# A gate block between two attention heads, half of two convolution channels by ScalarE and accumulating transfers, and a PSUM bank change in the last neighbourhood pair

## The chip, the cores and the metric

The kernel runs on one core of a Trainium2 chip. The metric is the device time of one execution in microseconds, as a median over repeated runs; beside it stands one execution that was taken with the hardware profiler. Engines are named as in the profile: PE (TensorE matmul), PEld (TensorE weight load), DVE (VectorE), ACT (ScalarE), POOL (GpSimd) and SP (SyncE, which issues most transfers). Times inside the profiled execution are microseconds from the start of its span. The two layers of the network are called the first and the second layer.

## The reference

The reference is a trunk of two layers over x of 512 tokens by 1024 channels. In each layer three token mixers run side by side on the same normalised input, a gate for each mixes them, and a SwiGLU FFN and a per-layer input embedding follow:

```python
h = rmsnorm(x, norm_mix[i])
proj = h @ w_in[i]
qa, ka, va, glu_in, qc, kc, vc, gates = jnp.split(proj, SPLITS, axis=-1)
ya = diff_attention(qa, ka, va, ...)          # 4 heads, two softmaxes each, a1 - lam * a2, then rmsnorm
yb = conformer_conv(glu_in, conv_w[i], ...)   # GLU, depthwise convolution of 31 taps over 512 channels, layernorm, silu
yc = neighbourhood_attention(qc, kc, vc, rpb[i])   # 8 heads, an 8 x 16 window on an 8 x 64 grid
ga, gb, gc = jnp.split(jax.nn.sigmoid(gates), 3, axis=-1)
merged = ga * (ya @ w_br_a[i]) + gb * (yb @ w_br_b[i]) + gc * (yc @ w_br_c[i])
x = x + merged @ w_o[i]
...
```

What matters here is the stretch of a layer from the neighbourhood attention to the gates: the convolution's depthwise taps are elementwise work that can run beside the matmuls at any time before `yb` is needed.

## The kernel before

Activations lie with channels on the 128 partitions and the 512 tokens along the free axis, so a projection's output block is a tile of 128x512 in one PSUM bank. Every fp32 product is emulated: both operands are split into a high and a low part in the fp32r type, and `mm3` (L181 to L183) issues three matmuls for each 128-deep chunk. A block of 1024 inputs is 8 chunks, 24 matmuls. Weights come in on SP's queue (`weights`, three buffers ahead), ACT copies the high part (L147) and DVE subtracts it for the low part (L161), so each weight tile puts about one 128x1024 instruction on ACT and on DVE. The helpers `split`, `tt`, `stt` and `act` record everything under their own lines: L147 is any ACT instruction, L161 any DVE tensor_tensor, L164 any DVE scalar_tensor_tensor; the tile names tell them apart.

PE runs its instructions in program order, and that order is written by hand: `layer` calls the blocks one after the other (`natten_in`, `natten_v`, `diff_in`, `diff_v`, `gate_c` and so on), and work that depends on softmax results is put into generators (`natten_unit`, `diff_unit`, `norm`) that are advanced by `tick`, once for every four chunks (twelve matmuls) that any projection issues. A `yield 2` means: go on two ticks later. So the pieces of one attention head stand a fixed number of matmuls apart among the projections of other blocks. On the other engines the order comes from the tile scheduler.

A head of the difference attention (`diff_in`, then four `diff_unit`s) does this: projections for Q and K, rope on DVE (tiles `diff_rp`: two multiplications, an addition and a split for each of Q and K), scores into `diff_sc`, a maximum on DVE (L910), two exponentials on ACT (`diff_a`, `diff_e`), the difference of the two on DVE (`diff_a`, L164), eight transposes on PE (L867, into two banks named `diff_tr`), their split by ACT and DVE into `diff_pt`, and the products with the values into `diff_av`. At the end of a head `norm` transposes the squares (L217), DVE sums them (L220, `diff_sm`), POOL raises to a power (L227, `diff_rc`), and PE transposes the result back over all partitions (L231) into a bank of the same two `tr` banks that the attention transposes use. PSUM has three `mm` banks, two `sc`, two `tr` and one `av`.

A neighbourhood unit ends in eight matmuls with the values (L752). Its result goes to the bank `av` for the first head of a pair and to an `mm` bank for the second; DVE then reads it into `natten_y`. `natten_v` projects the values; its four accumulators take two `mm` banks, the `av` bank and an `sc` bank, and eight reads by ACT and DVE (`natten_v`, `natten_x`) empty them.

The depthwise convolution has 4 channel blocks (`zs`) of 31 taps in a layer, one DVE instruction for each tap (L549 for the first of a block, then L164 into `conv_z`). `taps` yields them one by one, `background(after, n)` places n of them behind a given instruction (the table `BG` holds n for each kind of block), and `conv` issues those that are left. The accumulating form of a transfer is already in use in the FFN, where POOL adds one weight tile onto another (L995).

## Time and profile before

| what | value |
|---|---|
| median of 3 runs | 1779.75 us (1779.65 to 1779.84) |
| the profiled execution | 1779.11 us, of which its span is 1777.3 us and 1.8 us lie around it |
| mean granted clock of PE in it | 0.998 |
| PE, PEld | 1760.8 us (99%), 1544.1 us (87%) |
| DVE | 1413.5 us (80%), 2354 instructions |
| ACT | 893.4 us (50%), 1529 instructions |
| POOL | 97.4 us (5%), 114 instructions |
| transfers | 258.12 MB, mean 145 GB/s |

PE's durations overlap: a matmul of 128x512 is listed with 389 ns, but the next one starts about 227 ns after it (the modelled end reaches into the next), so PE's busy share hides short waits. Where a wait is measured here between two starts, the usual distance between them is taken off.

### The profile page before, as it was taken

To read this page: it belongs to the slowest core of one execution; us is meant where nothing else is said; L and a number is where in the kernel's file an instruction comes from. 1 tells how busy PE (TensorE), PEld (TensorE's weight loads), DVE (VectorE), ACT (ScalarE), POOL (GpSimd) and SP (SyncE) were. 2 spreads that over 40 slices of the span, in tenths; PEclk is the share of its full clock that TensorE was granted. 3 is DMA by queue.
4 is the path that set the end of the run, shared out by engine and by line. 5 is a ranking of instruction groups with operands and counts; after the bars stand their busy time and mean duration, and the time that the engine had idled before them with its cause. 6 is when DMAs were issued, how large, how long until landed. Compare 5 with 4: busy or idle time off the path is not lost.

```text
span 1777.3 us, 26765 instructions
## 1 busy us (share of the span) xinstructions
PE 1760.8 (99%) x9954; PEld 1544.1 (87%) x9954; DVE 1413.5 (80%) x2354; ACT 893.4 (50%) x1529; POOL 97.4 (5%) x114
## 2 busy tenths in 40 slices
PE   9999999999999999999999999999999999999998
PEld 7888878888899899998888887888888998989987
DVE  7967887998898587787776688779887985877776
ACT  5576555325565254454545765452356643534444
POOL 0000000000111010100000000000001110101000
PEclk9999999999999999999999999999999999999999
DMA  6577541334757366544446765423256673655332
GB/s 224 162 186 186 170 132 43 110 99 139 227 156 190 113 166 158 137 124 128 154 134 174 183 177 156 115 67 99 94 172 202 176 178 111 178 135 159 99 104 95
DMA packets 113698, 258.12 MB, mean 145 GB/s; under 512 B 14496, under 2 KB 23456, under 8 KB 113568
## 3 DMA queue, kind: packets, MB, share of 16 engines
q1 hardware_dynamic: 100176, 232.03, 42.7%
q0 software_dynamic: 12672, 23.07, 8.2%
q8 instruction: 78, 1.28, 0.3%
q10 hardware_dynamic: 720, 1.31, 0.2%
q14 instruction: 52, 0.43, 0.1%
HBM read 218.60 MB, written 7.34 MB: 127 GB/s over the span
## 4 chain that ended last, share of the span: by engine, by line
PE 90%; DVE 5%; ACT 1%; DMA 1%; issue 1%; SPq 0%; POOL 0%; ACTq 0%; DVEq 0%; POOLq 0%
PE ffn_mm L1025 4%; PE ffn_mm L1027 4%; PE ffn_mm L181 4%; PE ffn_mm L183 4%; PE ffn_mm L182 4%; PE ffn_mm L1026 4%; PE ffn_sc L1027 3%; PE ffn_sc L1025 3%; PE ffn_sc L1026 3%; PE mergea_mm L181 2%; PE mergea_mm L183 2%; PE mergea_mm L182 2%; PE gateb_mm L181 2%; PE wo_mm L181 2%; PE wo_mm L183 2%; PE wo_mm L182 2%
## 5 line engine op out<-in xcount | busy, mean ns | idle before, releaser
L164 DVE SCALAR_TENSOR_TENSOR conv_z<-glu_z,pre_par,conv_z 128x512 f32<-128x512 f32 x240 | 179.3, 747 | 3.0
L147 ACT ACTIVATE ffn_wh<-ffn_wr 128x1024 fp32r<-128x1024 f32 (+1 forms) x92 | 92.7, 1014 | 111.3 <-PE ffn_mm L182 80.7
L161 DVE TENSOR_TENSOR ffn_wl<-ffn_wr,ffn_wh 128x1024 fp32r<-128x1024 f32 (+1 forms) x92 | 107.3, 1172 | 5.4 <-ACT ffn_wh L147 4.9
L995 POOL DMA_DIRECT2D ffn_qk<-w_fu x88 | 77.9, 980 | 603.3 <-DMA ffn_qk<-w_fu 299.6
L161 DVE TENSOR_TENSOR ffn_t<-ffn_mm,wo_rb 128x512 f32<-128x512 f32 (+1 forms) x64 | 38.6, 604 | 67.8 <-PE ffn_mm L183 67.8
L147 ACT ACTIVATE mergea_wh<-mergea_wr 128x1024 fp32r<-128x1024 f32 (+1 forms) x32 | 27.1, 848 | 91.2 <-PE mergea_mm L182 71.7
L147 ACT ACTIVATE ffn_wh<-ffn_qk 128x1024 fp32r<-128x1024 f32 x44 | 46.7, 1061 | 36.7 <-PE ffn_mm L182 16.0
L161 DVE TENSOR_TENSOR ffn_wl<-ffn_qk,ffn_wh 128x1024 fp32r<-128x1024 f32 x44 | 53.8, 1223 | 10.8 <-ACT ffn_wh L147 10.8
L161 DVE TENSOR_TENSOR ffn_t<-ffn_t,ffn_t 128x512 f32<-128x512 f32 (+1 forms) x46 | 31.3, 680 | 32.0 <-ACT ffn_t L147 31.5
L161 DVE TENSOR_TENSOR diff_wl<-diff_wr,diff_wh 128x1024 fp32r<-128x1024 f32 x32 | 39.1, 1221 | 18.0 <-ACT diff_wh L147 12.4
L181 PE MATMUL ffn_mm<-ffn_v,ffn_wh 128*128 128x512 f32 x132 | 51.4, 389 | 0.0
L182 PE MATMUL ffn_mm<-ffn_v,ffn_wh 128*128 128x512 f32 x132 | 51.4, 389 | 0.0
L183 PE MATMUL ffn_mm<-ffn_v,ffn_wl 128*128 128x512 f32 x132 | 51.3, 389 | 0.0
L181 PE MATMUL ffn_mm<-ffn_y,ffn_wh 128*128 128x512 f32 x132 | 51.3, 389 | 0.0
L182 PE MATMUL ffn_mm<-ffn_y,ffn_wh 128*128 128x512 f32 x132 | 51.3, 389 | 0.0
L183 PE MATMUL ffn_mm<-ffn_y,ffn_wl 128*128 128x512 f32 x132 | 51.3, 389 | 0.0
L910 DVE TENSOR_REDUCE diff_s<-diff_sc 128x1 f32<-128x512 f32 x64 | 42.4, 683 | 10.0 <-PE diff_sc L819 10.0
L147 ACT ACTIVATE natten_e<-natten_e,natten_s 128x192 f32<-128x192 f32 (+1 forms) x88 | 39.3, 473 | 21.8 <-DVE natten_s L715 18.9
L1027 PE MATMUL ffn_mm<-wo_h,ffn_wl 128*128 128x256 f32 x176 | 49.8, 283 | 0.0
L1027 PE MATMUL ffn_sc<-wo_h,ffn_wl 128*128 128x256 f32 x176 | 49.8, 283 | 0.0
L1026 PE MATMUL ffn_mm<-wo_h,ffn_wh 128*128 128x256 f32 x176 | 49.8, 283 | 0.0
L1026 PE MATMUL ffn_sc<-wo_h,ffn_wh 128*128 128x256 f32 x176 | 49.8, 283 | 0.0
(882 smaller groups left out, 6477.3 us busy)
## 6 DMA issues: line engine op xcount, KB each, us to landing
ffn_qk<-w_fu POOLq DMA_DIRECT2D x88, 256.0 KB, 5.7
ffn_wr<-w_fg SPq DMA_DIRECT2D x44, 512.0 KB, 3.8
ffn_wr<-w_fd SPq DMA_DIRECT2D x32, 448.0 KB, 3.8
ffn_r<-w_fu SPq DMA_DIRECT2D x44, 256.0 KB, 4.3
ffn_qk<-w_fg SPq DMA_DIRECT2D x44, 256.0 KB, 4.0
ffn_qk<-w_fu SPq DMA_DIRECT2D x44, 256.0 KB, 4.4
natten_wr<-w_in SPq DMA_DIRECT2D x16, 512.0 KB, 4.1
diff_wr<-w_in SPq DMA_DIRECT2D x16, 512.0 KB, 3.8
```

Source lines behind the costliest of these rows:

```text
L147: i = self.nc.scalar.activation(out, in_, func, **kw)
L161: return self.nc.vector.tensor_tensor(out, a, b, op)
L164: return self.nc.vector.scalar_tensor_tensor(out, a, s, b, op0, op1)
L181: mm(out, wh, ah, start=first, stop=False)
L182: mm(out, wh, al, start=False, stop=False)
L183: mm(out, wl, ah, start=False, stop=last)
L910: nc.vector.tensor_reduce(out=m[:, u:u + 1], in_=sc, op=ALU.max, axis=AX.X, negate=True)
L995: nc.gpsimd.dma_start(q, wu[:, lo], accum_op=ALU.add)
L1025: mm(out, wh[:, c], bh, start=first and k == 0, stop=False, skip_group_check=True)
L1026: mm(out, wh[:, c], bl, start=False, stop=False, skip_group_check=True)
L1027: mm(out, wl[:, c], bh, start=False, stop=k == 3, skip_group_check=True)
```

## The change

Four things change, in both layers.

1. The second gate c block (`gate_c(acc, 1)`) is called between `diff_in(2)` and `diff_in(3)` instead of behind both. On PE the number of instructions stays (9745 rows); the 24 matmuls of that block now stand where the first projection of the last head stood, and that head's projections come 24 matmuls later.
2. For the third and fourth channel block of the convolution (`far`), the first nine taps each leave DVE. ACT multiplies the input by the tap (`conv_t`, 128x512; the first tap with the bias goes straight into the accumulator `conv_b`), and POOL issues a transfer from SBUF to SBUF that adds `conv_t` onto `conv_b` (256 KB, L575 of the changed kernel). That is 18 ACT instructions and 16 transfers in a layer; DVE's `taps` starts these two blocks at the tenth tap. `link` issues the next of the 18: two with each gate c block and one around each of two places between the heads.
3. The numbers of taps behind other blocks change: four instead of three at each weight tile of `natten_v`, none instead of one in the rope of a head, one instead of two at a gate c block, three instead of four in the merge.
4. In the last neighbourhood pair the second head's result goes to the `av` bank, like the first's, instead of to an `mm` bank.

Line numbers of the changed kernel are by 1 higher in the helpers (L161 is L162) and by 30 to 32 from `natten_unit` on (L867 is L899).

```diff
-BG = dict(glu=2, natten=1, values=3, diff=1, gatec=2, branchc=2, gateb=4, mergea=4, mergea2=2)
+BG = dict(glu=2, natten=1, values=4, diff=0, gatec=1, branchc=2, gateb=4, mergea=3, mergea2=2)
+LINKS = 18
...
-        self.todo = self.taps(zs, cs)
+        self.todo, self.links = self.taps(zs, cs), self.chain(zs)
...
         self.diff_in(2, sd, ya)
+        self.link()
+        self.gate_c(acc, 1)
         self.diff_in(3, sd, ya)
-        for m in range(1, KD):
+        self.link()
+        for m in range(2, KD):
             self.gate_c(acc, m)
...
-            c = self.sb("z", [P, 512])
+            if j < 2:
+                c, n = self.sb("z", [P, 512]), 0
+            else:
+                for _ in self.links:
+                    pass
+                c, n = self.far[j - 2], LINKS // 2
             cs.append(c)
-            for d in range(CON3W):
+            for d in range(n, CON3W):
...
+    def chain(self, zs):
+
+        self.far = [self.sb("b", [P, 512]) for _ in range(2)]
+        for n in range(LINKS):
+            d, j = divmod(n, 2)
+            w = self.par(self.i, "cw", (j + 2) * CON3W + d)
+            src = zs[j + 2].rearrange("p a b -> p (a b)")[:, d * GR:d * GR + 512]
+            if d == 0:
+                self.act(self.far[j], src, AF.Identity, scale=w, bias=self.par(self.i, "cb", j + 2))
+            else:
+                t = self.sb("t", [P, 512])
+                self.act(t, src, AF.Copy, scale=w)
+                self.nc.gpsimd.dma_start(self.far[j], t, accum_op=ALU.add)
+            yield
+
+    def link(self):
+
+        ph, self.phase = self.phase, "conv"
+        next(self.links, None)
+        self.phase = ph
...
-        av = self.ps(("av", "mm")[u])
+        av = self.ps("mm" if u and pr < 3 else "av")
...
         self.background(self.act(acc[m], ps, AF.Copy), self.bg["gatec"])
+        self.link()
+        self.link()
```

How the scheduler now places this is seen at three places. The first is DVE in the first layer, from the end of the first head's `norm` input to the two evacuations of the attention transposes (`diff_pt`). The names ending in 2139 and 2230 (`diff_rp`) are the ropes of the last head's Q and K. Before:

```order
L164 SCALAR_TENSOR_TENSOR diff_s_2278<-diff_s_2278,glu_nlam_445,diff_sm_1804 128x1
L161 TENSOR_TENSOR gatec_wl_2487<-gatec_wr_2485,gatec_wh_2486 128x1024
L161 TENSOR_TENSOR diff_rp_2139<-diff_rp_2139,diff_kh_2151 128x512
L161 TENSOR_TENSOR diff_rp_2230<-diff_rp_2230,diff_r_1315 128x512
L164 SCALAR_TENSOR_TENSOR conv_z_2147<-glu_z_324,pre_par_67,conv_z_2147 128x512
L161 TENSOR_TENSOR diff_rp_2231<-diff_rp_2231,diff_r_1317 128x512
L164 SCALAR_TENSOR_TENSOR diff_a_2283<-diff_e_2289,diff_s_2278,diff_a_2283 128x512
L161 TENSOR_TENSOR diff_rp_2230<-diff_rp_2230,diff_rp_2231 128x512
L161 TENSOR_TENSOR diff_pt_2311<-diff_tr_2306,diff_pt_2311 128x512
L161 TENSOR_TENSOR diff_pt_2319<-diff_tr_2314,diff_pt_2319 128x512
```

The same place after, from the sum of squares on (`diff_sm_2265`, L221):

```order
L221 TENSOR_REDUCE diff_sm_2265<-diff_tr_2260 128x4
L162 TENSOR_TENSOR diff_rp_2141<-diff_rp_2141,diff_r_1319 128x512
L162 TENSOR_TENSOR diff_rp_2142<-diff_rp_2142,diff_r_1321 128x512
L165 SCALAR_TENSOR_TENSOR diff_sm_2267<-diff_sm_2265,diff_sm_2225 128x4
L942 TENSOR_REDUCE diff_s_2271<-diff_sc_2272 128x1
L162 TENSOR_TENSOR diff_rp_2141<-diff_rp_2141,diff_rp_2142 128x512
L942 TENSOR_REDUCE diff_s_2271<-diff_sc_2278 128x1
L162 TENSOR_TENSOR diff_rp_2141<-diff_rp_2141,diff_kh_2151 128x512
L162 TENSOR_TENSOR gatec_wl_2501<-gatec_wr_2499,gatec_wh_2500 128x1024
L947 RECIPROCAL diff_s_2271<-diff_s_2271 128x1
L162 TENSOR_TENSOR diff_pt_2304<-diff_tr_2299,diff_pt_2304 128x512
```

One rope instead of two and no tap stand ahead of the first `diff_pt` now, and the difference `diff_a` of the next scores has moved behind both of them.

The second place is DVE at the end of `natten_v` in the first layer, where the accumulators are emptied (`natten_v`, `natten_x`; `conv_z_370` is the first block of the convolution). Before, from the first accumulator in an `mm` bank on:

```order
L161 TENSOR_TENSOR natten_v_697<-natten_mm_562,natten_v_697 64x4x128
L164 SCALAR_TENSOR_TENSOR conv_z_370<-glu_z_321,pre_par_67,conv_z_370 128x512
L161 TENSOR_TENSOR glu_wl_840<-glu_wr_838,glu_wh_839 128x1024
L161 TENSOR_TENSOR natten_v_697<-natten_mm_561,natten_v_697 64x4x128
L161 TENSOR_TENSOR natten_v_699<-natten_sc_564,natten_v_699 64x4x128
L161 TENSOR_TENSOR natten_v_698<-natten_mm_562,natten_v_698 64x4x128
L161 TENSOR_TENSOR natten_v_698<-natten_av_563,natten_v_698 64x4x128
L161 TENSOR_TENSOR natten_x_701<-natten_sc_564,natten_x_701 64x4x128
```

And after:

```order
L162 TENSOR_TENSOR natten_v_701<-natten_mm_562,natten_v_701 64x4x128
L165 SCALAR_TENSOR_TENSOR conv_z_370<-glu_z_321,pre_par_67,conv_z_370 128x512
L162 TENSOR_TENSOR glu_wl_844<-glu_wr_842,glu_wh_843 128x1024
L165 SCALAR_TENSOR_TENSOR conv_z_370<-glu_z_321,pre_par_67,conv_z_370 128x512
L162 TENSOR_TENSOR natten_v_701<-natten_mm_561,natten_v_701 64x4x128
L165 SCALAR_TENSOR_TENSOR conv_z_370<-glu_z_321,pre_par_67,conv_z_370 128x512
L162 TENSOR_TENSOR natten_v_703<-natten_sc_564,natten_v_703 64x4x128
L165 SCALAR_TENSOR_TENSOR conv_z_370<-glu_z_321,pre_par_67,conv_z_370 128x512
L162 TENSOR_TENSOR natten_v_702<-natten_mm_562,natten_v_702 64x4x128
L162 TENSOR_TENSOR natten_wl_925<-natten_wr_923,natten_wh_924 128x1024
L165 SCALAR_TENSOR_TENSOR conv_z_370<-glu_z_321,pre_par_67,conv_z_370 128x512
L162 TENSOR_TENSOR natten_x_705<-natten_sc_564,natten_x_705 64x4x128
```

Four taps and a weight split now stand between the weight split of `glu` and the last read of the `sc` bank, where four reads stood; one read (of the `av` bank) has moved behind it. In the second layer the eight reads stand in the same order as before, with no tap among them.

The third place is POOL's queue in the first layer. Before, the power of `glu`'s norm and those of the four heads (`diff_rc`) followed one another:

```order
L227 TENSOR_TENSOR glu_rc_317<-glu_sm_315,pre_power_104 128x4
L227 TENSOR_TENSOR diff_rc_2276<-diff_sm_2274,pre_power_104 128x4
L227 TENSOR_TENSOR diff_rc_2580<-diff_sm_2578,pre_power_104 128x4
L227 TENSOR_TENSOR diff_rc_2865<-diff_sm_2863,pre_power_104 128x4
L227 TENSOR_TENSOR diff_rc_3153<-diff_sm_3151,pre_power_104 128x4
```

After, up to the second head's power (`conv_b_1867` and `conv_b_1868` are the two accumulators):

```order
L575 DMA conv_b_1867<-conv_t_2163 128x512
L575 DMA conv_b_1868<-conv_t_2233 128x512
L575 DMA conv_b_1867<-conv_t_2236 128x512
L575 DMA conv_b_1868<-conv_t_2423 128x512
L228 TENSOR_TENSOR diff_rc_2269<-diff_sm_2267,pre_power_104 128x4
L575 DMA conv_b_1867<-conv_t_2492 128x512
L575 DMA conv_b_1868<-conv_t_2495 128x512
L575 DMA conv_b_1867<-conv_t_2566 128x512
L575 DMA conv_b_1868<-conv_t_2569 128x512
L228 TENSOR_TENSOR diff_rc_2600<-diff_sm_2598,pre_power_104 128x4
```

Each transfer waits for the landing of the one before it on the same accumulator and for its own ACT instruction. The first head's power stands behind four transfers, the second head's behind eight, the third head's behind all sixteen, and so does the fourth's. On ACT, the instructions for transfers two to six (`conv_t_2233` to `conv_t_2495`) stand five in a row right behind the two that read the first head's `diff_av` (`diff_ss`, `diff_t`). The `conv_t` tiles share their seven buffers with `diff_t`, so later ones wait until an earlier transfer has landed.

## The prediction

> **What bounds the kernel now.** The page first: PE is busy for nearly the whole span, so only its waits can be won.
>
> ```profile
> span 1777.3 us, 26765 instructions
> PE 1760.8 (99%) x9954; PEld 1544.1 (87%) x9954; DVE 1413.5 (80%) x2354; ACT 893.4 (50%) x1529; POOL 97.4 (5%) x114
> L164 DVE SCALAR_TENSOR_TENSOR conv_z<-glu_z,pre_par,conv_z 128x512 f32<-128x512 f32 x240 | 179.3, 747 | 3.0
> ```
>
> The span is 1777.3 us of an execution of 1779.11 us. The change moves about 18 taps a layer off DVE, 2 x 18 x 0.747 = 26.9 us of DVE time. That is worth nothing by itself: DVE is at 80%, and what counts is where PE waits for DVE. So next the waits of PE:
>
> ```profile
> PE diff_tr L231 <- DVE diff_pt L161: 6.0, 2, 3.0
> PE diff_mm L614 <- DVE natten_y L161: 1.1, 2, 0.7
> PE natten_mm L752 <- ACT diff_wh L147: 1.0, 2, 0.5
> PE diff_tr L867 <- DVE diff_a L164: 0.9, 2, 0.5
> PE gateb_mm L181 <- ACT gateb_kh L147: 0.3, 2, 0.2
> PE natten_av L752 <- DVE natten_a L161: 0.3, 1, 0.3
> ```
>
> All lie in the stretch that the change touches, most of them once in each layer, and they add up to 9.6 us. That is the most that can be won beside the clock. The largest is the transpose of the first head's `norm` (L231). PE's timeline there, in the first layer:
>
> ```profile
> 220.02 0.60 PE L217 MATMUL diff_tr<-pre_ident,diff_ss 128*128 128x128 f32 x4
> 227.32 0.39 PE L182 MATMUL gatec_mm<-glu_h,gatec_wh 128*128 128x512 f32 x1
> 227.55 0.39 PE L183 MATMUL gatec_mm<-glu_h,gatec_wl 128*128 128x512 f32 x1
> 230.95 0.62 PE L231 MATMUL diff_tr<-pre_ident,diff_rc 128*128 128x128 f32 x4 [3.02 <-DVE diff_pt L161]
> ```
>
> Matmuls start 0.23 us apart (227.32 to 227.55), so L231 could have started at 227.78 and lost 230.95 - 227.78 = 3.17 us. It waits for a `tr` bank, which is free when DVE has done the first `diff_pt`. What DVE did between the sum of squares (start 220.65) and that:
>
> ```profile
> 220.65 0.69 DVE L220 TENSOR_REDUCE diff_sm<-diff_tr 128x4 f32<-128x512 f32 x1 [1.42 <-PE diff_tr L217]
> ...
> 225.25 1.23 DVE L161 TENSOR_TENSOR gatec_wl<-gatec_wr,gatec_wh 128x1024 fp32r<-128x1024 f32 x1
> 226.39 0.68 DVE L161 TENSOR_TENSOR diff_rp<-diff_rp,diff_kh 128x512 fp32r<-128x512 f32 x1
> 226.99 0.68 DVE L161 TENSOR_TENSOR diff_rp<-diff_rp,diff_r 128x512 f32<-128x512 f32 x1
> 227.59 0.74 DVE L164 SCALAR_TENSOR_TENSOR conv_z<-glu_z,pre_par,conv_z 128x512 f32<-128x512 f32 x1
> ...
> 230.12 1.28 DVE L161 TENSOR_TENSOR diff_pt<-diff_tr,diff_pt 128x512 fp32r<-128x512 f32 x2
> ```
>
> DVE has no gap there: its queue, not a dependence, sets 230.12. An instruction of 128x512 costs 0.60 us from start to start (226.39 to 226.99), a tap 0.67, a weight split 1.14. Last the granted clock (third field from the end), in the first layer's wait and behind the second layer's:
>
> ```profile
> 228.00:232.00 4.00, 1.05 (x7) 0.99 (x8) 4.00 (x8) 0.63 (x1) 0.00 (x0) 1.00 0.88 204
> 1109.50:1113.00 3.50, 3.29 (x10) 2.83 (x11) 3.10 (x6) 1.39 (x3) 0.00 (x0) 0.53 0.86 238
> ```
>
> Both layers wait equally long, but only behind the second wait does PE run 3.5 us at 0.53: that costs up to 3.5 x 0.47 = 1.6 us.
>
> **The change part by part.**
>
> *The first head's stall.* In the new order DVE has, between the same sum of squares and the first `diff_pt`: four rope steps, two maxima, one weight split and two small instructions. From 220.65: seven instructions of 0.60 (the sum of squares with them) and the small one make 224.9, if nothing holds them. But the last rope step and the weight split wait for ACT, which now takes `diff_a`, `diff_kh`, the weight copy, `diff_e` and `diff_pt` in that order. ACT's prices and the start of its chain:
>
> ```profile
> 217.15 0.28 PE L183 MATMUL diff_av<-diff_pt,diff_v 128*128 128x256 f32 x1
> 217.47 0.60 ACT L147 ACTIVATE diff_ss<-diff_av 128x512 f32<-128x512 f32 x1
> 217.96 0.68 ACT L147 ACTIVATE diff_t<-diff_av,glu_subg 128x512 f32<-128x512 f32 x1
> 218.53 0.60 ACT L147 ACTIVATE diff_rp<-diff_mm 128x512 f32<-128x512 f32 x1
> 221.98 0.69 ACT L147 ACTIVATE diff_a<-diff_sc,diff_s 128x512 f32<-128x512 f32 x1 [2.85 <-DVE diff_s L910]
> ...
> 222.66 0.68 ACT L147 ACTIVATE diff_e<-diff_sc,diff_s 128x512 f32<-128x512 f32 x1
> ...
> 224.15 1.06 ACT L147 ACTIVATE gatec_wh<-gatec_wr 128x1024 fp32r<-128x1024 f32 x1 [0.73 <-ACT diff_e L147]
> ```
>
> The five `conv_t` run from 218.5, 0.56 us apart, until 221.4, before the first maximum is there. That maximum ends at about 223.2; then `diff_a` 0.68 (221.98 to 222.66), `diff_kh` 0.56, the copy 1.0, `diff_e` 0.68 and `diff_pt` 0.6 give 226.7, and DVE's half of `diff_pt` 0.68 more: 227.4. PE arrives at 227.78. There are eight hand-overs between ACT and DVE, which cost some hundredths each, so I leave 0.2 us of the 3.17: 2 x -2.97 = **-5.9**. Bounds: 0 and 0.8 us left in each layer, so -6.3 to -4.7. The gate block behind `diff_in(2)` costs PE nothing: the same 24 matmuls in another place.
>
> *The clock.* With the wait gone the slow stretch should go: **-1.4**, between -1.6 and 0 (another wait could set it off). The Trainium skill ("TensorE: Matmul & The Clock Gate", Part 1) says that the throttle judges activity in free-running windows of 3413 ns and knows only half and full rate. By that rule the first layer's equal wait was lucky in its phase, so a wait of 3 us that comes back could cost the clock twice; the trace's 0.53 over 3.5 us agrees.
>
> *The last neighbourhood pair.* L614, the projection of the values, waits for `natten_y` because it gets the `mm` bank that the pair's second head used. Now it doesn't: **-1.1** (0 to -1.5). In exchange the second head waits for the single `av` bank. In the first layer DVE reads that bank out by 171.3 and the next product starts at 174.53:
>
> ```profile
> 170.61 0.69 DVE L161 TENSOR_TENSOR natten_y<-natten_y,natten_av 64x512 fp32r<-64x512 f32 x1
> 174.53 0.88 PE L752 MATMUL natten_mm<-natten_pt,natten_v 128*128 128x256 f32 x6
> ```
>
> so nothing is lost.
>
> *The difference `diff_a` before L867.* Two taps stand ahead of it before, 1.3 us, and none after; the wait of 0.9 in two should go: **-0.9** (-0.3 to -0.9). The waits at L752 and at gate b stay, since as much is moved in front of them as is taken away.
>
> *Four taps more in the first layer's `natten_v`.* Here the change adds to DVE where DVE is full:
>
> ```profile
> 74.83 1.22 DVE L161 TENSOR_TENSOR glu_wl<-glu_wr,glu_wh 128x1024 fp32r<-128x1024 f32 x1
> ...
> 78.96 0.69 DVE L161 TENSOR_TENSOR natten_x<-natten_sc,natten_x 64x512 fp32r<-64x512 f32 x1
> 81.13 0.28 PE L711 MATMUL natten_sc<-natten_qk 128*128 128x256 f32 x1
> ...
> 956.96 0.69 DVE L161 TENSOR_TENSOR natten_x<-natten_sc,natten_x 64x512 fp32r<-64x512 f32 x1
> 960.56 0.31 PE L711 MATMUL natten_sc<-natten_qk 128*128 128x256 f32 x1
> ```
>
> The second half of the first scores (L711, 81.13) needs the `sc` bank that `natten_x` empties. After `glu_wl` (done at 76.05) now come four taps, three reads and a weight split: 4 x 0.67 + 3 x 0.72 + 1.14 = 6.0 (a read is 0.69 long), so `natten_x` starts at 82.0 and ends at 82.7: PE waits 1.55 us. The later wait of 0.3 at L752 should vanish in that: **+1.25** (0.5 to 2.0). In the second layer the reads keep their order and end 3 us ahead of PE (956.96 against 960.56): nothing.
>
> *The accumulating transfers.* POOL's queue is otherwise empty, but the heads' powers now stand behind transfers. The nearest rows are the FFN's accumulating transfers, of the same 256 KB, and the power:
>
> ```profile
> L995 POOL DMA_DIRECT2D ffn_qk<-w_fu x88: 862/883/1243, 453.9 to 1643.7; - x88
> DMA to landing us min/median/max: 3.9/5.7/8.6
> L227 POOL TENSOR_TENSOR diff_rc<-diff_sm,pre_power x8: 1006/1007/1017, 222.1 to 1199.3; 128x4 f32<-128x4 f32 x8
> ```
>
> With a landing time D: the second transfer is issued when its `conv_t` is done, at 219.1; the fourth waits for that landing and holds POOL 0.9 us; then the power takes 1.0. It is ready at 221.0 + D, for the median at 226.7, 1.1 us ahead of PE. So **0**, and from D = 6.8 on a wait. I take the median, since the weight stream loads the transfer engines no less in the FFN. The Trainium skill ("DMA: Bandwidth & Descriptors", Anatomy of one DMA) gives 2.0 us plus bytes over 436 GB/s, an estimate of 2.6 us here. By that page the power would be ready 4 us early; the rows above are twice as slow, and I go by them. DVE's tail of the convolution has no wait of PE, and the last landing is long past when DVE goes on from it.
>
> The sum: -5.9 - 1.4 - 1.1 - 0.9 + 1.25 = -8.05. From 1779.11 this is 1771.1; the median lies 0.64 above the profiled execution, so **1771.7**. The best ends of all terms give -6.3 - 1.6 - 1.5 - 0.9 + 0.5 = -9.8 (1769.9), the worst -4.7 + 0 + 0 - 0.3 + 2.0 = -3.0 (1776.8).
>
> **The rivals.** (The bound of no change is 0.2%, 3.56 us, about what a measurement of this kernel can tell.)
>
> *A: POOL's queue takes the place of DVE's.* For: 5.7 us is a median, and 8.6 occurs; the transfers form a chain, and a transfer behind a slow one starts late. At D = 8.6 the first head waits 1.8 us in each layer: 1771.7 + 3.6 = 1775.3. It ends on the other side when the third head's power is late as well:
>
> ```profile
> 251.45 0.28 PE L183 MATMUL diff_av<-diff_pt,diff_v 128*128 128x256 f32 x1
> 293.58 0.49 PE L231 MATMUL diff_tr<-pre_ident,diff_rc 128*128 128x128 f32 x3
> ```
>
> With the first stall gone, these fall 3.2 us earlier. The ninth transfer goes at about 250.5 after the second head's product, four landings follow one after another, then two issues and the power: 250.5 + 4D + 2.8, needed at 290.4. That decides from D = 9.3. At D = 10 it is 2 x 3.2 for the first head and 2 x 2.9 for the third: 1771.7 + 12.2 = 1783.9, slower; at 12 some 1803. Against: no row of 88 is over 8.6.
>
> *B: the stall only moves.* ACT is a chain of hand-overs now; if `diff_e` or the weight copy comes late, L231 waits 2 us instead of 0.2, and the slow clock may stay: 1771.7 + 3.6 + 1.4 = 1776.7. For: by my working the chain ends only 0.4 us ahead of PE. Against: DVE's own work would be done by 226.1 (224.9, a weight split of 1.14 and a small one), so one late hand-over is not added to a full queue.
>
> *C: a wait that the trace of before doesn't show*, for instance a gate c weight tile that now is due 24 matmuls earlier on SP's queue, eats most of it: 1777 to 1782.
>
> **How the numbers follow.** The forecast 0.62 (1769.9 to 1776.8, almost all of it faster); B 0.13, half of it within the bound; A up to D = 9.3 0.10, mostly still faster; A beyond 0.08, slower; C 0.07, mostly within the bound. Faster: 0.60 + 0.06 + 0.08 = 0.74; slower 0.08 + 0.02 = 0.10; the same 0.16. The range leaves out A beyond and part of C on top, and on the low side whatever I haven't seen: 1768.5 to 1779.5.
>
> **What would show it.** L231 leaves the list of PE's waits or stands there with under 0.5 us each; a new line of `natten_sc` on DVE `natten_x` of 1 to 2 us, once; no stretch at 0.5 of the clock behind the first head; landings of the new transfers near 5.7 us. A wait of L231 on POOL `diff_rc` would make A right, a wait on `diff_pt` of 2 us B. A time over 1779.5 would make the sum wrong, not its sizes.

## The result, and the profile after

The changed kernel takes 1776.63 us (median of 18 runs, 1774.15 to 1778.3), beside 1779.27 us for the kernel before on the same chips (18 runs). The ratio is 0.9984, with a 95% interval of 0.9977 to 0.9991: 2.6 us faster, 0.16%, where 8 us were forecast. The profiled execution took 1777.74 us, 1.1 over its median, with a span of 1775.9.

The waits of PE after (engine, line, what it waited for; us in all, times, longest):

```profile
PE diff_av L183 <- DVE diff_pt L162: 1.9, 2, 1.2
PE natten_sc L741 <- DVE natten_x L162: 1.7, 1, 1.7
PE diff_sc L851 <- ACT diff_e L148: 1.5, 2, 0.9
...
PE natten_mm L782 <- DVE natten_a L162: 0.9, 2, 0.5
PE diff_tr L232 <- DVE diff_pt L162: 0.8, 2, 0.4
PE diff_mm L182 <- DVE natten_y L162: 0.5, 2, 0.3
```

The three waits that the sum took away are gone: the first head's L231 (6.0 us), L614 (1.1) and L867 (0.9). The line of L232 that still stands there is another head's. Around the first head's transpose, PE's, DVE's and POOL's timelines of the first layer:

```profile
229.60 0.39 PE L184 MATMUL diff_mm<-glu_h,diff_wl 128*128 128x512 f32 x1
229.83 0.60 PE L232 MATMUL diff_tr<-pre_ident,diff_rc 128*128 128x128 f32 x4
...
228.81 0.67 DVE L162 TENSOR_TENSOR diff_pt<-diff_tr,diff_pt 128x512 fp32r<-128x512 f32 x1
...
227.00 1.39 POOL L228 TENSOR_TENSOR diff_rc<-diff_sm,pre_power 128x4 f32<-128x4 f32 x1
```

L232 follows the matmul before it by the usual 0.23 us. DVE had freed the bank at 229.48, 0.35 us ahead of PE, and POOL's power was ready at 228.4, 1.4 us ahead. But five waits of the list are new: `diff_av`, `natten_sc`, `diff_sc` on ACT's `diff_e`, L232 in the second head, and L182 on `natten_y`. With `natten_sc` the clock came along. Windows of the changed kernel (the granted clock is the third field from the end):

```profile
82.00:86.00 4.00, 3.96 (x13) 3.27 (x14) 3.89 (x13) 2.56 (x9) 0.00 (x0) 0.60 0.57 193
1106.00:1110.00 4.00, 4.00 (x21) 3.21 (x20) 4.00 (x10) 2.19 (x5) 2.00 (x3) 1.00 1.03 209
```

The slow stretch of the second layer is gone, and in this execution one has come up in the first layer, behind the new wait.

Counted from start to start of PE's matmuls (with the usual distance taken off, both layers together), the two profiles compare so:

| place | before | after |
|---|---|---|
| first head's L231 | 6.35 | 0 |
| value projection waits for `natten_y` (L614) | 1.46 | 0 |
| L867 waits for `diff_a` | 1.26 | 0 |
| L752 waits for `natten_a` (first layer, first unit) | 0.45 | 0 |
| `natten_sc` waits for `natten_x` (first layer) | 0 | 1.87 |
| `diff_av` waits for `diff_pt`, second head | 0 | 2.17 |
| `diff_sc` waits for `diff_e`, first head | 0 | 1.86 |
| second head's L232 waits for `diff_pt` | 0 | 1.14 |
| `diff_mm` waits for `natten_y` of the third pair | 0 | 0.87 |
| half clock behind a wait | about 1.6 | about 1.6 |

The last row comes from comparing the slowed matmuls with the same ones at full clock (in the other layer before, in the kernel with the bank undone after). Beside it, 9.5 us went and 7.9 came. That is the 1.4 us by which the spans differ, to within a fraction.

### The profile page after: what moved, and what is told of

Same layout as the page of the kernel before. It is cut to its first block, busy times and chain, and to the rows that moved or that the text cites. A ratio compares the mean times of both kernels' runs of the same rounds, so it can differ in the third digit from the quotient of the medians.

```text
span 1775.9 us, 26835 instructions
## 1 busy us (share of the span) xinstructions
PE 1761.1 (99%) x9954; PEld 1542.6 (87%) x9954; DVE 1392.7 (78%) x2318; ACT 913.0 (51%) x1565; POOL 126.7 (7%) x146
## 4 chain that ended last, share of the span: by engine, by line
PE 91%; DVE 4%; DMA 2%; ACT 1%; issue 1%; SPq 1%; POOL 0%; ACTq 0%; DVEq 0%; POOLq 0%
PE ffn_mm L1057 4%; PE ffn_mm L1059 4%; PE ffn_mm L182 4%; PE ffn_mm L183 4%; PE ffn_mm L184 4%; PE ffn_mm L1058 4%; PE ffn_sc L1059 3%; PE ffn_sc L1057 3%; PE ffn_sc L1058 3%; PE mergea_mm L184 2%; PE mergea_mm L182 2%; PE mergea_mm L183 2%; PE gateb_mm L182 2%; PE wo_mm L182 2%; PE wo_mm L184 2%; PE wo_mm L183 2%
## 5 line engine op out<-in xcount | busy, mean ns | idle before, releaser
L162 DVE TENSOR_TENSOR ffn_wl<-ffn_wr,ffn_wh 128x1024 fp32r<-128x1024 f32 (+1 forms) x92 | 107.4, 1173 | 5.4 <-ACT ffn_wh L148 4.7
L162 DVE TENSOR_TENSOR ffn_t<-ffn_mm,wo_rb 128x512 f32<-128x512 f32 (+1 forms) x64 | 38.7, 605 | 67.7 <-PE ffn_mm L184 67.7
L165 DVE SCALAR_TENSOR_TENSOR conv_z<-glu_z,pre_par,conv_z 128x512 f32<-128x512 f32 x120 | 89.7, 748 | 1.2
L165 DVE SCALAR_TENSOR_TENSOR conv_b<-glu_z,pre_par,conv_b 128x512 f32<-128x512 f32 x88 | 65.9, 749 | 1.7
L575 POOL DMA_DIRECT2D conv_b<-conv_t x32 | 29.7, 974 | 492.8 <-ACT conv_b L148 246.5
L162 DVE TENSOR_TENSOR ffn_wl<-ffn_qk,ffn_wh 128x1024 fp32r<-128x1024 f32 x44 | 53.8, 1224 | 10.8 <-ACT ffn_wh L148 10.8
L162 DVE TENSOR_TENSOR ffn_t<-ffn_t,ffn_t 128x512 f32<-128x512 f32 (+1 forms) x46 | 31.3, 680 | 31.9 <-ACT ffn_t L148 31.4
L162 DVE TENSOR_TENSOR diff_wl<-diff_wr,diff_wh 128x1024 fp32r<-128x1024 f32 x32 | 39.1, 1222 | 16.9 <-ACT diff_wh L148 10.9
L182 PE MATMUL ffn_mm<-ffn_v,ffn_wh 128*128 128x512 f32 x132 | 51.4, 389 | 0.0
L182 PE MATMUL ffn_mm<-ffn_y,ffn_wh 128*128 128x512 f32 x132 | 51.3, 389 | 0.0
```

Source lines behind the costliest of these rows:

```text
L162: return self.nc.vector.tensor_tensor(out, a, b, op)
L165: return self.nc.vector.scalar_tensor_tensor(out, a, s, b, op0, op1)
L182: mm(out, wh, ah, start=first, stop=False)
L575: self.nc.gpsimd.dma_start(self.far[j], t, accum_op=ALU.add)
```

## The experiments

The theory was that the forecast gain is real and that each new wait belongs to one part of the change. The main rival was that the accumulating transfers slow what runs beside them, by POOL's queue or by load. The kernels below each differ from the changed kernel or from the kernel before by the lines shown. Times are medians; since the chips differ, the distance to the kernel before measured beside it is given as well.

**Three taps in `natten_v` again.**

```diff
-BG = dict(glu=2, natten=1, values=4, diff=0, gatec=1, branchc=2, gateb=4, mergea=3, mergea2=2)
+BG = dict(glu=2, natten=1, values=3, diff=0, gatec=1, branchc=2, gateb=4, mergea=3, mergea2=2)
```

> The changed kernel with three taps instead of four at each weight tile of natten_v, all else as changed. Theory (each new wait belongs to one part of the change): the wait of natten_sc on natten_x in the first layer, 1.7 us in the changed kernel's profile, leaves the list of PE's waits, and with it the half clock behind it; the time falls by 1.9 us, and by about 3.3 where the half clock had followed: 1773.3 to 1774.7 if the changed kernel is at 1776.6. Rival (the accumulating transfers slow everything they run beside): the wait goes, others grow, the time stays within 0.5 us of the changed kernel.

1781.92 us, 2.3 above the kernel before. Its waits:

```profile
PE conv_tr L609 <- ACT conv_rp L148: 3.8, 2, 1.9
PE diff_av L183 <- DVE diff_pt L162: 2.0, 2, 1.4
```

The `natten_sc` wait is gone, but both expectations miss: a wait at the convolution's mean (`conv_tr`, 2.1 us in each layer by start to start) shows that the tail has no room. Four taps fewer in `natten_v` are four taps more at the end, and PE reaches that end while DVE is still at it. So the taps that the links take off DVE only make up for those that the table takes away from the rope, the gate c blocks and the merge; the fourth tap in `natten_v` is needed.

**The bank undone.**

```diff
-        av = self.ps("mm" if u and pr < 3 else "av")
+        av = self.ps(("av", "mm")[u])
```

> The changed kernel with the last pair's second head in an mm bank again; the order on ACT and DVE is the same as in the changed kernel. Theory: the waits of diff_sc on diff_e (1.5 us in two) come from the order on ACT, where natten_y now stands behind diff_kh, and not from the bank; the value projection of the difference attention waits for natten_y again, 1.5 to 2.5 us in each layer, since natten_y is later than before, and the diff_sc wait shrinks by as much as PE is held up ahead of it. Time 1 to 3 us above the changed kernel. Rival (the single av bank delays natten_y and so diff_e): the diff_sc waits go, and the time is 0 to 2 us below the changed kernel.

1777.92 us, 1.7 below the kernel before (ratio 0.9991, 0.9982 to 1.0).

```profile
PE diff_mm L644 <- DVE natten_y L162: 3.2, 2, 1.8
PE natten_sc L741 <- DVE natten_x L162: 1.7, 1, 1.7
```

As the theory had it: the order on ACT and DVE is that of the changed kernel, and the wait for `natten_y` at the value projection is three times that of before, with the `diff_sc` wait gone, since PE comes later. The time differs from the changed kernel's by less than the two intervals can tell apart; the verdict rests on these lines.

**No links.**

```diff
-LINKS = 18
+LINKS = 0
```

> The changed kernel without ACT taps and accumulating transfers: DVE does all 31 taps of the third and fourth block. Theory: the wait of the second head's norm transpose on diff_pt (0.8 us in two) goes, the first head's stall stays away, since what moved it was the gate block and the rope without taps; DVE has 27 us more to do, but later, in the merge, where PE does not wait for it: time from 1 us below to 1 us above the changed kernel, unless the tail of the convolution shows a new wait. Rival (the transfers cost by POOL's queue or by load on the transfer engines): 4 us or more below the changed kernel.

1803.31 us, 23.7 above the kernel before.

```profile
PE conv_tr L609 <- ACT conv_rp L148: 27.5, 2, 13.8
```

The waits of the second head's L232 and of `diff_av` are gone, so the links do have a part in them, and the first head's stall stays away without links. But 18 taps more in the tail are 13.8 us of waiting in each layer: what the theory had named as an exception is what decides, and its main figure is far off.

**The gate block behind both heads again.**

```diff
         self.link()
-        self.gate_c(acc, 1)
         self.diff_in(3, sd, ya)
         self.link()
-        for m in range(2, KD):
+        for m in range(1, KD):
```

> The changed kernel with the second gate c block behind both heads again. Theory: the wait of diff_av on diff_pt (1.9 us in two) goes, because the last head's rope no longer meets the second head's attention transposes on DVE; the first head's norm transpose waits again, by 1 to 2 us in each layer (3.2 less the two or three taps that are gone). Time from 0 to 2 us above the changed kernel. Rival (the taps, not the gate block, made the first stall): the first head's wait stays under 0.3 us, the diff_av wait goes, time 2 us below the changed kernel.

1777.32 us, 2.3 below the kernel before (0.9989, 0.9981 to 0.9998).

```profile
PE diff_tr L232 <- DVE diff_pt L162: 3.9, 2, 2.2
PE natten_sc L740 <- DVE natten_x L162: 1.7, 1, 1.7
PE diff_sc L850 <- ACT diff_e L148: 1.6, 2, 0.9
```

The first head's wait is back with about two thirds of its size, and the second head's waits are gone. Within the rest of the change, then, the gate block takes 4.2 us of waiting (by start to start) from the first head and puts 3.3 on the second. What is left at the first head is in part a wait of DVE: ahead of `diff_pt` it stands still for 1.09 us in the first layer and 1.49 in the second, at a step of the rope that needs the landing of a transfer (`diff_rp`).

**Taps behind the rope and in `natten_v` as before, the rest as changed.**

```diff
-BG = dict(glu=2, natten=1, values=4, diff=0, gatec=1, branchc=2, gateb=4, mergea=3, mergea2=2)
+BG = dict(glu=2, natten=1, values=3, diff=1, gatec=1, branchc=2, gateb=4, mergea=3, mergea2=2)
```

> The changed kernel with three taps at a weight tile of natten_v and one behind each rope step's first multiplication, as before; links, gate block and bank stay as changed. Theory: the order on ACT (natten_y ahead of diff_kh) is as before, so the diff_sc waits on diff_e (1.5 us) and most of the diff_mm waits on natten_y are gone; the natten_sc wait (1.7 us) is gone; four more taps in a layer are done before the tail, so the tail's wait (2 us in each layer with three taps in natten_v alone) is gone too. Some of the first or second head's wait on diff_pt comes back, up to 1 us in each layer. Time 2 to 4 us below the changed kernel: 1772.5 to 1774.5. Rival (no arrangement gains: whatever is taken off one place of DVE's queue turns up at the next): within 1 us of the changed kernel.

1776.08 us, 3.9 below the kernel before (0.9979, 0.9970 to 0.9988).

```profile
PE diff_tr L899 <- DVE diff_a L165: 1.3, 2, 0.7
...
PE diff_tr L232 <- DVE diff_s L165: 0.6, 2, 0.3
PE diff_av L183 <- DVE diff_pt L162: 0.6, 2, 0.3
```

The `natten_sc` wait is gone and no tail wait has come, as the theory had it, and the `diff_sc` wait shrank to 0.5 us in one. But smaller waits, and L899 on `diff_a`, took most of it back, so the time missed the theory's 1772.5 to 1774.5. By the distances to the kernel before it is 1.25 us below the changed kernel, between the theory and the rival.

**The gate block alone, on the kernel before.**

```diff
         self.diff_in(2, sd, ya)
+        self.gate_c(acc, 1)
         self.diff_in(3, sd, ya)
-        for m in range(1, KD):
+        for m in range(2, KD):
```

> The kernel before with the second gate c block between the last two heads and nothing else: no links, all taps where they were, the old bank. Theory: the first head's norm transpose (6.3 us by start to start) loses most of its wait, and about half comes back at the second head's diff_pt, as in the changed kernel; L614 and diff_a waits stay. Time 2 to 4 us below the kernel before. Rival (the taps behind the rope and the links made the stall go): the first head's wait stays above 2 us in each layer, time within 1 us of before.

1773.18 us (1772.88 to 1773.69), 6.8 below the kernel before (0.9963, 0.9950 to 0.9975): more than expected, and 4.15 us better than the whole change by these distances.

```profile
PE diff_mm L615 <- DVE natten_y L161: 1.3, 2, 0.9
PE diff_tr L231 <- DVE diff_pt L161: 1.1, 2, 0.6
```

The first head's wait falls from 3.17 to 0.72 us in each layer, nothing turns up in the second head, and the half clock is gone. So the `diff_av` wait of the changed kernel does not belong to the gate block by itself. DVE's timelines show the difference, first in the changed kernel, then with the gate block alone:

```profile
243.14 1.29 DVE L162 TENSOR_TENSOR diff_rp<-diff_rp,diff_r 128x512 f32<-128x512 f32 x2 [1.75 <-DMA diff_rp<-diff_rp]
...
246.75 1.29 DVE L162 TENSOR_TENSOR diff_rp<-diff_rp,diff_r 128x512 f32<-128x512 f32 x2
...
248.55 0.69 DVE L162 TENSOR_TENSOR diff_rp<-diff_rp,diff_rp 128x512 f32<-128x512 f32 x1
249.15 1.29 DVE L162 TENSOR_TENSOR diff_pt<-diff_tr,diff_pt 128x512 fp32r<-128x512 f32 x2
```

```profile
243.57 0.67 DVE L161 TENSOR_TENSOR diff_pt<-diff_tr,diff_pt 128x512 fp32r<-128x512 f32 x1
244.16 0.68 DVE L161 TENSOR_TENSOR diff_rp<-diff_rp,diff_rp 128x512 f32<-128x512 f32 x1
...
244.89 0.68 DVE L161 TENSOR_TENSOR diff_pt<-diff_tr,diff_pt 128x512 fp32r<-128x512 f32 x1
```

In the changed kernel, without taps between its steps, the last head's rope runs as one piece, and the scheduler puts it ahead of both `diff_pt`; with the gate block alone the `diff_pt` are let in between. (The missing taps don't decide this by themselves: the kernel below that puts them behind the gate c blocks lets the `diff_pt` in as well.) Nor is that order the whole cause. The kernel without links has it too, and there PE does not wait at `diff_av`:

```profile
238.97 1.29 DVE L162 TENSOR_TENSOR diff_rp<-diff_rp,diff_r 128x512 f32<-128x512 f32 x2
...
244.99 1.28 DVE L162 TENSOR_TENSOR diff_pt<-diff_tr,diff_pt 128x512 fp32r<-128x512 f32 x2
```

What differs is the first line of the changed kernel's timeline. A rope step multiplies a copy of the tile with its blocks of partitions exchanged, which transfers on SP's queue make. DVE stands still for 1.75 us (2.58 in the second layer) until such a transfer has landed, with the rest of its queue behind it. Without links it waits 0 and 0.31 us there. PE loses what goes beyond about 1 us:

| kernel | DVE waits for the rope's transfer (first, second layer) | PE waits at `diff_av` |
|---|---|---|
| changed | 1.75, 2.58 | 0.80, 1.37 |
| three taps in `natten_v` | 1.77, 2.46 | 0.82, 1.53 |
| bank undone | 0.94, 1.62 | 0, 0.69 |
| no links | 0, 0.31 | 0, 0 |

The wait for `natten_y` of the third pair goes the same way, with a rope step some 7 us ahead of it. In the changed kernel DVE waits there 1.50 and 1.44 us for the transfer and PE loses 0.4 in each layer; with the gate block behind both heads 2.11 and 1.24 us cost 1.1 and 0; without links 0.27 and 1.09 cost nothing. So both waits need the links, and most of them the rope without taps as well: with the taps back in the rope 0.9 us is left at `diff_av` and none for `natten_y`. The main rival, then, has a share in the loss. How the links make those transfers late isn't shown. In the first layer the last of the eight ahead of the `diff_av` wait was issued 1.0 us later beside PE's transposes than without links, and their median from issue to landing was 4.7 us instead of 3.2.

**The gate block and the bank, on the kernel before** (the two edits above).

> The kernel before with the gate block moved and the last pair's bank changed; no links, all taps where they were. Theory: as the gate block alone, and the L614 wait (1.5 us by start to start) goes without a new one, since the order on ACT is as before: 1 to 1.5 us below the gate block alone, 3.5 to 5.5 us below the kernel before, and so below the changed kernel. Rival (the accumulating transfers are what frees PE): 2 us or more above the changed kernel.

1773.58 us, 6.4 below the kernel before (0.9965, 0.9953 to 0.9978). The part on the changed kernel came true, the part on the bank didn't.

```profile
PE diff_tr L868 <- DVE diff_a L164: 1.3, 2, 0.7
PE diff_tr L231 <- DVE diff_pt L161: 1.1, 2, 0.6
```

The wait at the value projection has left the list, but `diff_a` is waited for longer, and one unit of the second layer waits longer for `natten_a`: PE, which comes earlier, meets DVE busy. The bank is worth nothing here that the intervals could tell.

**The gate block and the links, taps and bank as before** (`link`, `chain` and `taps` as in the change, `BG` and the bank of the kernel before).

> The kernel before with the gate block moved and the 18 ACT taps and 16 accumulating transfers a layer added; taps behind other blocks and the bank as before. Beside the gate block alone (1773.2) this shows what the links cost by themselves. Theory: ACT's conv_t stand in front of the exponentials, the weight copies and diff_pt of the first and the second head, which PE waits for: 0.4 to 0.6 us at each of two places in each layer, together 1.5 to 2.5 us above the gate block alone, and the runs spread further. Rival (the links cost nothing, and the changed kernel loses by its table of taps alone): within 0.5 us of the gate block alone.

1785.75 us, 6.0 above the kernel before (1.0035, 1.0022 to 1.0047) and so 12.8 above the gate block alone.

```profile
PE diff_tr L232 <- POOL diff_rc L228: 9.2, 4, 3.3
```

Neither expectation has this: PE waits for POOL. Two of the four waits are the first head's, 3.5 us each by start to start, and a stretch at half clock comes with each of them. The other two are the last head's, 1.45 us each; there POOL itself waits for DVE's sums (`diff_sm`). POOL's timeline in the first layer, at the first head:

```profile
219.18 1.76 POOL L575 DMA_DIRECT2D conv_b<-conv_t  x2 [73.61 <-ACT conv_t L148]
223.08 0.89 POOL L575 DMA_DIRECT2D conv_b<-conv_t  x1 [2.14 <-DMA conv_b<-conv_t]
224.57 0.87 POOL L575 DMA_DIRECT2D conv_b<-conv_t  x1 [0.60 <-ACT gatec_wh L148]
228.35 0.86 POOL L575 DMA_DIRECT2D conv_b<-conv_t  x1 [2.92 <-DMA conv_b<-conv_t]
228.91 1.36 POOL L228 TENSOR_TENSOR diff_rc<-diff_sm,pre_power 128x4 f32<-128x4 f32 x1
```

In this arrangement the scheduler puts six transfers ahead of the first head's power instead of four, and the sixth waits for the landing of one that itself had waited. The power comes at 230.3, while PE is there at 226.9. This is rival A of the prediction, its mechanism and its place, in another kernel; in the changed kernel, with the power behind four transfers, POOL is in time by 1.4 us.

**The gate block and four taps in `natten_v`.**

```diff
-BG = dict(glu=2, natten=1, values=3, diff=1, gatec=2, branchc=2, gateb=4, mergea=4, mergea2=2)
+BG = dict(glu=2, natten=1, values=4, diff=1, gatec=2, branchc=2, gateb=4, mergea=4, mergea2=2)
```

> The kernel before with the gate block moved and four taps instead of three at a weight tile of natten_v, nothing else. Theory: the first layer's natten_sc waits 1.6 to 1.9 us for natten_x; in some executions the half clock follows, for 1.4 us more, so the runs spread over 1.5 us or more where the gate block alone spreads over 0.8. Median 1.4 to 2.8 us above the gate block alone. Rival (that wait is swallowed by later ones): within 0.5 us of it.

1774.91 us (1774.04 to 1775.23), 4.8 below the kernel before: 1.7 above the gate block alone, or 1.95 by the distances to the kernel before.

```profile
PE natten_sc L712 <- DVE natten_x L161: 1.7, 1, 1.7
PE diff_tr L868 <- DVE diff_a L164: 1.4, 2, 0.7
```

The wait of the fourth tap is confirmed (1.86 us by start to start), and the time lies where the theory had it, though the intervals of the two kernels overlap. The spread is 1.2 us and no half clock followed in the profile, so the clock's part was not seen here.

**The taps of the rope, put elsewhere.** Three kernels ask what these eight taps a layer do. The first takes them from the kernel before and puts them nowhere else (`diff=0` in its table); it ran once.

> The kernel before without the taps behind the rope (eight in a layer go to the tail). Theory: the taps' removal by itself turns the order on ACT, natten_y behind diff_kh, so PE waits for natten_y at the value projection for longer than before (1.5 to 2.5 us in each layer instead of 0.6 to 0.9), with no other part of the change present; the convolution's tail waits for DVE, since it has eight taps more, 3 to 6 us in each layer. Rival (links or bank turn the order): the waits at the value projection are as before.

1786.03 us.

```profile
PE conv_tr L579 <- ACT conv_rp L147: 9.2, 2, 4.6
PE diff_mm L614 <- DVE natten_y L161: 2.2, 2, 1.2
```

The theory's points hold, though the wait for `natten_y` stays a little below its range: the tail waits, and that wait grows from 1.46 to 2.50 us (by start to start, both layers) without any other part of the change. What neither foresaw is that L231 has left the list: taking the taps out of the rope is enough by itself to clear the first head's stall, as the gate block nearly is. Beside the rest of the change it is not: the kernel with the gate block behind both heads has no taps in its rope either, and keeps 4.2 of the 6.35 us.

The second moves the gate block and puts the eight taps behind the gate c blocks (`diff=0, gatec=3`).

> The kernel before with the gate block moved and the eight taps of a layer that stand behind rope steps put behind the gate c blocks instead (three each). Theory: the first head's remaining wait (1.4 us in two by start to start) and the waits for diff_a (1.2 us in two) go, the order on ACT turns as it does whenever the rope loses its taps, so the value projection waits for natten_y 0.5 to 0.7 us longer in each layer: within 1.5 us of the gate block alone, on either side. Rival (taps behind a gate block meet the attention transposes as the rope does): new waits of diff_pt of 1 us or more in each layer, 1 to 3 us above it.

1772.52 us (1772.01 to 1773.6), 7.2 below the kernel before (0.9960, 0.9947 to 0.9972).

```profile
PE diff_mm L615 <- DVE natten_y L161: 2.2, 2, 1.2
PE diff_tr L231 <- DVE diff_pt L161: 1.3, 2, 0.6
```

It is level with the gate block alone, as expected, and the waits for `diff_a` are gone, but the first head's wait did not go (0.79 us in each layer for 0.72). No tap stands on DVE between the sum of squares and `diff_pt` there; the difference `diff_a` (0.75 us) now stands ahead of both `diff_pt`.

The third keeps the taps in the first two heads' rope and puts the other four behind the last gate blocks.

```diff
-        self.background(self.act(acc[m], ps, AF.Copy), self.bg["gatec"])
+        self.background(self.act(acc[m], ps, AF.Copy), self.bg["gatec"] + (m > 3))
...
-            self.background(self.tt(raw, raw, st["tabs"][0], ALU.mult), self.bg["diff"])
+            self.background(self.tt(raw, raw, st["tabs"][0], ALU.mult), self.bg["diff"] if head < 2 else 0)
```

> The kernel before with the gate block moved, the taps behind the rope kept for the first two heads and dropped for the last two, and the four taps so freed put behind the last four gate c blocks. Theory: the order on ACT (natten_y ahead of diff_kh) stays, since the first two ropes keep their taps, so the value projection waits no longer than with the gate block alone; what is left of the first head's wait (1.4 us in two) shrinks by a tap or two, 0 to 0.7 us left in each layer; the tail has as many taps as before and does not wait. Time 0 to 1.4 us below the gate block alone: 1771.8 to 1773.2. Rival (the remaining wait is ACT's chain, not DVE's queue): within 0.3 us of it.

1771.81 us (1771.07 to 1772.38), 7.8 below the kernel before (0.9955, 0.9941 to 0.9969).

```profile
PE natten_mm L753 <- ACT diff_wh L147: 1.0, 2, 0.5
PE diff_tr L868 <- DVE diff_a L164: 1.0, 2, 0.5
PE diff_mm L615 <- DVE natten_y L161: 0.8, 2, 0.4
```

L231 is off the list and nothing has come in its place. It has the lowest median of all, 5.2 us below the changed kernel by their distances to the kernel before; from the gate block alone the intervals do not separate it.

## Why the prediction was wrong

The direction was right, and the time lies inside the stated range; the size was wrong, 2.6 us for 8.05. By the prediction's own bound of 3.56 us this counts as no change, to which it gave 0.16.

- *The first head's stall.* Right: 6.35 us went, 5.9 were forecast. The chain by way of ACT ended 0.35 us ahead of PE, where I had 0.4.
- *L614 and `diff_a`.* Both waits went as forecast, by somewhat more (1.46 and 1.26 us by start to start for 1.1 and 0.9). "So nothing is lost" was wrong all the same. Two places on, PE waits for `diff_e` (1.86 us). The timeline of ACT after shows why:

```profile
183.46 0.69 ACT L148 ACTIVATE diff_a<-diff_sc,diff_s 128x512 f32<-128x512 f32 x1 [1.59 <-DVE diff_s L942]
...
184.13 1.05 ACT L148 ACTIVATE diff_wh<-diff_wr 128x1024 fp32r<-128x1024 f32 x1
185.08 0.68 ACT L148 ACTIVATE diff_e<-diff_sc,diff_s 128x512 f32<-128x512 f32 x1
```

  A weight copy stands between the two exponentials, and `natten_y`, which had moved behind `diff_kh`, stands between the two maxima on DVE. The kernel with the bank undone has the same order, and there PE loses the time at the value projection instead; the kernel before without taps in its rope has the late `natten_y` too. So the table of taps turned the order, and the bank only chose where it is paid.
- *Four taps in `natten_v`.* Right in place, and near in size: 1.87 us less the 0.45 that vanished behind it, 1.42 for 1.25.
- *The clock.* The second layer's slow stretch went, as forecast; it had cost 1.6 us where the sum has 1.4. "Another wait could set it off" came true in the profiled execution, behind `natten_sc`, so the term's upper bound of 0 held there. That it makes the median's share I can't say: the kernel with that wait and no other new one did not show it.
- *The gate block "costs PE nothing".* Wrong in the changed kernel, where it meets a rope without taps whose transfers come late beside the links (2.17 us at `diff_av`); right where it stands alone.
- *The accumulating transfers: 0.* POOL was in time, and the landing was shorter than taken (median 4.4 us for 5.7). But I followed the links on POOL's queue only. The rope's transfers on SP's queue came later with them, which the sum does not have. And on ACT, ahead of the second head's weight copy, they cost:

```profile
255.02 2.58 ACT L148 ACTIVATE conv_t<-glu_z,pre_par 128x512 f32<-128x512 f32 x4
257.47 0.71 ACT L148 ACTIVATE diff_a<-diff_sc,diff_s 128x512 f32<-128x512 f32 x1
...
258.79 0.75 ACT L148 ACTIVATE conv_t<-glu_z,pre_par 128x512 f32<-128x512 f32 x1
259.41 1.09 ACT L148 ACTIVATE gatec_wh<-gatec_wr 128x1024 fp32r<-128x1024 f32 x1
```

  The maximum of the scores was there at 256.8, and `diff_a` came at 257.47; the fifth `conv_t` took another 0.6 us ahead of the weight copy, and behind that DVE's weight split and `diff_pt` came late (1.14 us at L232).
- *"DVE's tail of the convolution has no wait of PE".* True after, since its taps are about as many as before, but by less room than I thought. The table takes 20 taps of a layer away from blocks ahead of the tail (24 behind rope, gates and merge, less 4 in `natten_v`) and the links take 18. Without the links the tail waits 13.8 us in each layer.

The step that failed is the one behind the sum: I priced the new order of ACT and DVE only at the places where PE had waited before, and took all other places for free ("costs PE nothing", "so nothing is lost", and 0 for the transfers). Of the 7.9 us that came, 6.0 arose at four places where PE had not waited (`diff_av`, `diff_sc`, the second head's L232, the third pair's `natten_y`), all of them within reach of taps, links or the gate block. Of the rivals, A's mechanism is real but did not decide here; B came true in its kind, though not at the place where I put it: the stall moved to the next head. Of these 6.0 us, 3.0 (`diff_av` and `natten_y`) are absent without the links and shrink to 0.9 with the taps back in the rope, and 1.1 (L232) are absent without the links. How the whole 4.15 us between the gate block alone and the change divides between links and table stays open, since no run has the whole of one alone without a new loss: the links without the table push POOL's power back, and the table without the links lets the tail wait.

## What to carry to other kernels

Where an engine's queue is full, a stall can be cleared by moving one block of the waiting engine's own work in front of it; that took two lines here and was worth more than the whole change. Work taken off a full engine need not pay: here the scheduler filled the gaps with steps that other waits depend on, among them steps that stood waiting for a transfer with the whole queue behind them. So follow the new order at every place where the critical engine reads from it, not only at those where it waited before. And before taking background work out of its slots, ask what its deadline has to spare: here four taps were too many.

## What the runs showed of the hardware

The accumulating transfers of 256 KB from SBUF to SBUF landed after 3.2, 4.4 and 8.9 us (least, median, most of 32), those of the FFN from HBM after 3.5, 5.8 and 8.7; each of the first kind kept POOL for 0.87 us (median; 2.08 at most), and a power of the heads, 1.01 us before, took up to 2.19 us beside them.

A stretch at half clock followed waits of PE as short as 1.87 us, but not each time: one of the five profiles with the `natten_sc` wait of 1.86 to 1.87 us shows it, one of the two layers with 2.08 us at `conv_tr`, one of the two with 3.17 us at L231, and all six stalls of 3.5 to 13.9 us; none follows the 1.83 and 2.35 us at L232 with the gate block behind both heads. Up to stalls of 3.5 us it lasted 3.41 us and cost about 1.6 us; with the stalls of 4.7 us it lasted 6.8 us, and with those of 13.9 us 13.7 and 17.1. The Trainium skill ("TensorE: Matmul & The Clock Gate", Part 1) has free-running windows of 3413 ns; that fits a wait that trips it only in some phases. The traces agree: in each profile the clock changes only whole multiples of 3.413 us apart, 323 of them (1102.5 us) from its first rise to the half clock in the kernel before and 23 (78.5 us) in the changed kernel.
